# Squares of the queries as a moving operand: float32r products with a column of ones, and a transfer that turns the sums into columns

## The chip, the cores and the metric

The kernel runs on one core of a Trainium2 chip. The metric is the device time of one execution in microseconds. TensorE (PE) multiplies: it loads a stationary operand (PEld, weights of up to 128 x 128) and streams a moving operand of up to 512 columns through it into a PSUM bank. VectorE (DVE), ScalarE (ACT) and GpSimd (POOL) do the elementwise work, and SyncE (SP) issues most transfers. Each engine executes its own instructions in order and waits on semaphores for the others.

## The reference, cut to what matters

A layer of an encoder is applied to a prompt of 1024 tokens and a sample of 256 tokens. The part that the change touches is the gated delta rule: convolved and SiLU-activated queries, keys and values, four heads of 128 channels, normalised queries and keys, a recurrence in each direction, and a norm over each head's output.

```python
q = l2norm(heads(q, DN_DK))          # q * rsqrt(sum(q*q) + EPS)
...
o_f = gated_delta_chunked(q, k, v, g_f, beta_f)
o_b = flip(gated_delta_chunked(flip(q), flip(k), flip(v), flip(g_b), flip(beta_b)))
o = jnp.transpose(o_f + o_b, (0, 2, 1, 3))
o = rmsnorm(o, norm_w) * jax.nn.silu(gate.reshape(bsz, seq, DN_HEADS, DN_DV))
```

The output of the recurrence is linear in the query, and a norm follows. The kernel therefore leaves the query unscaled and carries its sum of squares, `ssq`, into the norm's epsilon: the norm needs the mean of o squared plus EPS times (128 times) the query's own sum of squares plus its epsilon. So one number per token and head is wanted: the sum over 128 channels of the query squared.

## The kernel before, in words

Activations lie with channels on the 128 partitions and tokens along the free dimension. Large projections are made in three products of split operands: `split` writes a rounded float32r copy (`hi`, ACT) and the remainder (`lo`, VectorE or GpSimd), and `mm3` multiplies hi by hi, hi by lo and lo by hi. Products of the recurrence itself are in plain f32.

The recurrence is done in five batches of 8 blocks of 128 tokens: bi = 0 to 3 are the heads of the prompt, bi = 4 the four heads of the sample. Each batch is a generator, `dn_batch`, that runs beside the main work: the projections of the convolution (`conv_tile`), of the gates (`gate_tile`, `gate_pair`) and, for the last batch, of the memory (`mem_k`, `mem_v`). A planner (`Trunk`) interleaves them in the program text. It keeps a clock that each product advances by its estimated time (`mm`: columns / 2.4 ns for float32r with at least 256 columns, four times that for f32, 2 ns for an f32 product of one column). A side generator yields a number of ns, and is continued when the clock has gone that far. TensorE executes in the order of this text (`manual_schedule`); the order of the other engines is made by the framework's scheduler from the data that each instruction needs, so an instruction on ACT or VectorE may stand earlier or later than its place in the text.

Within a batch, in order of the text:

1. decays from `grd` (L759 to L777), in the buffers `gb0` and `gb1`, which become the two directions' matrices X;
2. the blocks of 32 of the triangular inverse, by VectorE alone (L838, L841), between round trips through DRAM that rearrange them (`xsd`, `usd`, `vsd`); L844 copies the result out for the transfers L850 and L851;
3. values and keys transposed (L864, L867), and the flag "vw" that lets the main work go on;
4. the squares of the queries (L871 to L879): in each of two halves ACT squares 128 x 512 (L874), the generator yields SQ = 1800, and four f32 products take the squares as the stationary operand and the column `one` as the moving one, which gives the sums as columns, tokens on the partitions. VectorE adds the epsilon and scales (L879);
5. X[0] becomes X[0] + X[1] (L884); four buffers of the inverse are cleared (L889); SP brings back the 32 x 32 blocks (L897, L898 into `uc`, L901 and L902 into `UTm` and `Um`, L905 into `U`); after 2500 ns ACT copies `uc` into the odd blocks of `UTm` and `Um` (L911) and, after EXP / 2 = 2000 ns (in batch 0 another 5500), into `U` (L914); after another 2000 ns come the products of the inverse's two levels. The first of them takes X[0] and `UTm` (in the profile bank<-UT,gb), VectorE masks it (L924), the next takes `Um` (bank<-UT,zt), and VectorE adds it to `U` (L932). Between the levels `Mt` takes the buffer `gb1` (L943), is transposed, and fills the new `UTm` and `Um` (L950, L952);
6. the scan over the blocks, and then the norm: L1032 combines the sums of squares of the output with `ssq`, three Newton steps take the root, and the planner leaves ROOT = 2500 ns (16000 in batch 3) before the scaled output is used.

The buffers `gs` (three of 128 x 514) are shared: by the convolution's tanh (L693), its sample block (L688, L690), the evacuation of the gates (L1051, written to DRAM from there), the squares, and the final output. Weights come by SP (`load`, L135) into `raw` and are split by ACT (L125) and VectorE (L126). ACT takes the projections out of PSUM for the convolution (L723, L727, L731) and starts it (L688); VectorE continues it (L690, L695).

Of the kernel before, what the change touches and what calls it, by code (L numbers as in the profile page):

```python
# [8 lines left out]
F32 = mybir.dt.float32  # L9
F32R = mybir.dt.float32r  # L10
I32 = mybir.dt.int32
AF = mybir.ActivationFunctionType
ALU = mybir.AluOpType
# [4 lines left out]
P = 128  # L18
D = 1024
KT = D // P  # L20
NP, NS = 1024, 256
# [5 lines left out]
EPS = 1e-6  # L27
# [14 lines left out]
def f32(ap):  # L42
    return ap.bitcast(F32)


def quad(ps):
    return ps.rearrange("p (c t) -> p c t", t=P)
# [7 lines left out]
class Trunk:  # L55
# [44 lines left out]
    def mm(self, out, l, r, start=True, stop=True, more=False):  # L100
        n = 1
        for x in out.shape[1:]:
            n *= x
        if l.dtype == F32R:
            self.clock += max(n, 16) / 2.4 * (1 if n >= 256 else 4)
        else:
            self.clock += (4 * n / 2.4) if n > 1 else 2
        self.nc.tensor.matmul(out, l, r, start=start, stop=stop, skip_group_check=more)  # L108
# [10 lines left out]
    def tr(self, out, x, ident):  # L119
        self.clock += 64  # L120
        self.nc.tensor.transpose(out, x, ident)  # L121
# [42 lines left out]
def trunk_kernel(ctx: ExitStack, tc: tile.TileContext, a):  # L164
    nc = tc.nc
    V, S, G, T, SY = nc.vector, nc.scalar, nc.gpsimd, nc.tensor, nc.sync
    K = Trunk(ctx, tc, a)
    mm, mm3, tr, split = K.mm, K.mm3, K.tr, K.split

    def pool(name, bufs=1, **kw):  # L170
        if kw.get("space") != DRAM:
            kw["reuse_waits"] = "tile"
        return tc.tile_pool(name=name, bufs=bufs, **kw)
# [7 lines left out]
    dp = ctx.enter_context(pool("dram", space=DRAM))  # L181
# [5 lines left out]
    n = 0  # L187
# [29 lines left out]
    one = cst[:, C_ONE : C_ONE + 1]  # L217

    def bank(p=pq, tag="b"):
        return p.tile([P, 512], F32, tag=tag, name="bank")  # L220
# [4 lines left out]
    def rsqrt(y, x, scratch):  # L225
        V.tensor_scalar(out=y.bitcast(I32), in0=x.bitcast(I32), scalar1=-0.5, scalar2=float(0x5F3759DF), op0=ALU.mult, op1=ALU.add)
        for _ in range(3):
            V.scalar_tensor_tensor(out=scratch, in0=y, scalar=-0.5, in1=x, op0=ALU.mult, op1=ALU.mult)
            V.tensor_tensor(out=scratch, in0=scratch, in1=y, op=ALU.mult)
            V.scalar_tensor_tensor(out=y, in0=scratch, scalar=1.5, in1=y, op0=ALU.add, op1=ALU.mult)  # L230
# [167 lines left out]
    squares = hp.tile([P, 4, 1024], F32, tag="lo0", name="squares")  # L398
# [5 lines left out]
    parts = []  # L404
    for k in range(0, KT, 2):
        sq = xp.tile([P, 512], F32, tag="nacc" if k == 0 else "nsq", name="first", bufs=2 if k == 0 else 3)
# [6 lines left out]
    ms, y = pb[:, :NS], pb[:, NS : 2 * NS]  # L413
    parts = [t[:, i * NS : (i + 1) * NS] for t in parts for i in range(2)]
# [10 lines left out]
    hi, lo = x_h[2]  # L425
    rooms = [bank() for _ in range(3)]
    los = []
    for k in range(KT):
        if k in (5, 7):
            t = xp.tile([P, 512], F32, tag="nsq", name="nt", bufs=3)[:, :NS]  # L430
        else:
            at = min(k, 5)
            t = rooms[at % 3][:, at // 3 * NS : at // 3 * NS + NS]
# [3 lines left out]
        while los and (k == KT - 1 or los[0][0] < k):  # L437
            n, t = los.pop(0)
# [229 lines left out]
    qp = des.enter_context(pool("dn"))  # L668


    for i, (x, y) in enumerate(((0, 2), (1, 3), (0, 1), (2, 3))):
        V.scalar_tensor_tensor(out=mine[:, i : i + 1], in0=bdm[:, x : x + 1], scalar=-1.0, in1=bdm[:, y : y + 1], op0=ALU.mult, op1=ALU.subtract)
    def gs():
        return qp.tile([P, 514], F32, tag="gs", name="gs", bufs=3)

    def conv_tile(kind, h, out):
# [6 lines left out]
        def conv(raw, dst, n):  # L683
            for j in range(5):
                wj = sm[:, wc + j : wc + j + 1]
                src = raw[:, j : j + n]
                if j == 0:
                    S.activation(dst, src, AF.Copy, scale=wj)  # L688
                else:
                    V.scalar_tensor_tensor(out=dst, in0=src, scalar=wj, in1=dst, op0=ALU.mult, op1=ALU.add)  # L690
                yield CONV
            t = gs()[:, :n]
            S.activation(t, dst, AF.Tanh, scale=0.5)  # L693
            yield CONV
            V.scalar_tensor_tensor(out=dst, in0=t, scalar=1.0, in1=dst, op0=ALU.add, op1=ALU.mult)  # L695

        def after():
            for b, n in ((0, 510), (1, 514)):
                while len(raws) <= b:
                    yield 300  # L700
                yield from conv(raws[b], acc[:, 510 * b : 510 * b + n], n)
            out.append(quad(acc))
            while len(raws) < 3:
                yield 300
            smp = gs()[:, :NS]
            yield from conv(raws[2], smp, NS)
            SY.dma_start(sqd[kind, h], smp)
# [9 lines left out]
        for b, (t0, n) in enumerate(BLOCKS):  # L717
# [11 lines left out]
            else:  # L729
                raw = new_raw(0, 258)  # L730
                S.activation(raw[:, 2 : 2 + n], ps, AF.Copy)  # L731
                raws.append(raw)

    xsd = [dp.tile([2, 8, 4, 32, 32], F32, name=f"xsd{i}") for i in range(5)]
    usd = [dp.tile([2, 2, 8, P, 2, 16], F32, name=f"usd{i}") for i in range(5)]
    vsd = [dp.tile([2, 2, 8, 64, 2, 32], F32, name=f"vsd{i}") for i in range(5)]

    def big(tag, bufs=1):
        return qp.tile([P, 8, P], F32, tag=tag, name=tag, bufs=bufs)

    flags = set()
# [5 lines left out]
    def dn_batch(bi, qkv, chains):  # L747
# [4 lines left out]
        q2, k2 = qkv[:2]  # L752
# [29 lines left out]
        ssk, ssq, r, scr, r2, iv = (cw[:, i] for i in (0, 1, 2, 3, 6, 7))  # L782
# [4 lines left out]
        for b in range(8):  # L787
            V.scalar_tensor_tensor(
                out=junk, in0=pg[b // 4][:, (b % 4) * P : (b % 4 + 1) * P], scalar=1.0, in1=ident, op0=ALU.mult, op1=ALU.mult,
# [23 lines left out]
        X = dec  # L813
# [20 lines left out]
        for i in range(30, -1, -1):  # L834
            n, c = 32 - i, (i + 1) // 2
# [3 lines left out]
                out=t3, in0=u3[:, c:, i:],  # L839
                in1=XL[:, 32 * i + i : 32 * i + 32].unsqueeze(1).to_broadcast([P, m, n]), op=ALU.mult)  # L840
# [27 lines left out]
            yield 1000  # L868
        flags.add(("vw", bi))

        pc = bank()  # L871
        for hf in range(2):
            sq = quad(gs()[:, :512])
            S.activation(sq, q2[:, 4 * hf : 4 * hf + 4, :], AF.Square)  # L874
            yield SQ
            for c in range(4):
                n = 4 * hf + c
                mm(pc[:, n : n + 1], sq[:, c, :], one)
        V.tensor_scalar(out=ssq, in0=pc[:, :8], scalar1=4.0 * EPS, scalar2=EPS * P, op0=ALU.add, op1=ALU.mult)  # L879

        V.tensor_tensor(out=X[0], in0=X[0], in1=X[1], op=ALU.add)  # L884
        Xs = X[0]
        U = [big(f"U{d}") for d in range(2)]
        Um, UTm = big("UT1"), big("UT0")
# [11 lines left out]
        for s in (0, 2):  # L899
            c = slice(16 * s, 16 * s + 16)  # L900
            SY.dma_start(own(UTm, s), vsd[bi][1, 0][:, c].rearrange("b c h j -> (c h) b j"))  # L901
            SY.dma_start(own(Um, s), vsd[bi][0, 1][:, c].rearrange("b c h j -> (c h) b j"))  # L902
        for s in range(4):
            c = slice(16 * s, 16 * s + 16)
# [14 lines left out]
        for level, mask in enumerate((m64, m128)):  # L919
            for hf, hs in enumerate(halves):  # L920
                pz = bank()
                for c in range(4):
                    mm(pz[:, c * P : (c + 1) * P], Xs[:, hs.start + c, :], UTm[:, hs.start + c, :])
                V.tensor_tensor(out=zts[:, hf], in0=quad(pz), in1=mask.unsqueeze(1).to_broadcast([P, 4, P]), op=ALU.mult)  # L924
                yield LEV
            yield LEV
            for hf, hs in enumerate(halves):
                pu = bank()
                for c in range(4):
                    mm(pu[:, c * P : (c + 1) * P], zts[:, hf, c, :], Um[:, hs.start + c, :])  # L930
                for d in range(2):
                    V.scalar_tensor_tensor(  # L932
                        out=U[d][:, hs, :], in0=quad(pu), scalar=mine[:, 2 * level + d : 2 * level + d + 1], in1=U[d][:, hs, :],
                        op0=ALU.mult, op1=ALU.add)
                yield LEV
            if level:
                break

            Mt, Um, UTm = big("gb1"), big("UT1"), big("UT0")
            lo64, hi64 = slice(0, 64), slice(64, P)  # L940
            for hs in halves:
                for q, d in ((lo64, 0), (hi64, 1)):
                    S.activation(Mt[q, hs, :], U[d][q, hs, :], AF.Copy)  # L943
                yield LEV
            yield LEVT
            for hs in halves:
                pt = bank()
                for c in range(4):
                    tr(pt[:, c * P : (c + 1) * P], Mt[:, hs.start + c, :], ident)
                S.activation(UTm[:, hs, :], quad(pt), AF.Copy)  # L950
                for q, d in ((lo64, 1), (hi64, 0)):
                    G.tensor_copy(Um[q, hs, :], U[d][q, hs, :])  # L952
                yield LEV
            yield LEV
# [72 lines left out]
        sso, ms, t_ = cw[:, 4], cw[:, 5], cw[:, 19]  # L1027
        for b in range(8):
            junk = sq128("vt", 4)
            S.activation(junk, o[:, b, :], AF.Square, accum_out=sso[:, b : b + 1])  # L1030
            yield 250
        V.scalar_tensor_tensor(out=ms, in0=sso, scalar=1.0 / P, in1=ssq, op0=ALU.mult, op1=ALU.add)  # L1032
        rsqrt(t_, ms, sso)
        yield ROOT[bi]
        V.tensor_tensor(out=o, in0=o, in1=t_.unsqueeze(2).to_broadcast([P, 8, P]), op=ALU.mult)
# [633 lines left out]
    for h in range(HEADS):  # L1669
# [26 lines left out]
        if h == HEADS - 1:  # L1696
# [12 lines left out]
            for b in range(3):  # L1709
                hi, lo = o_h[b]  # L1710
# [5 lines left out]
    op = OutProj(o_h, h3)  # L1716
# [664 lines left out]
FILL = ((0, 0, 5), (0, 0, 4), (0, 0, 4), (0, 0, 0))  # L2381
FIRST = 12000
LANE = 1.05
SQ, EXP, LEV, LEVT, SCAN = 1800, 4000, 500, 1000, 1000
SC1, SC2, SC3 = 1200, 700, 700
TAIL, ROOT, FIRST_EXP = 3000, (2500, 2500, 2500, 16000, 2500), 5500
YA = 4500
# [88 lines left out]
```

## Time and profile before

| what | us |
|---|---|
| median of three runs | 2191.11 (2189.59 to 2192.89) |
| the profiled execution, its own time | 2190.45 |
| its span, first to last instruction | 2188.7 |
| ACT busy in the span | 879.9 |
| VectorE busy in the span | 1354.3 |

Granted TensorE clock: 0.999 of full speed over the span. The lines of the page and of the trace are shown in the prediction, each where it is used. In a group's line "x80 | 9.5, 239" means eighty instructions, 9.5 us busy in total and 239 ns the mean of one. In a timeline a line is start, length, engine, line of the kernel, operation, output and inputs, count, and in brackets how long the engine had been idle and what ended that. The names of tiles are those of the program's allocations: `gs` is also the square, `cst` the column `one`, `acc` the convolution's output, `UT` is `UTm` or `Um`, `gb` is X.

### The profile page before, as it was taken

The numbers are of one execution on the slowest core, as the hardware profiler recorded it, in microseconds if no ns is written. First come the engines' busy times: TensorE is split into PE (matmuls) and PEld (weight loads), VectorE is DVE, ScalarE is ACT, GpSimd is POOL, SyncE is SP. The second block draws the span as 40 slices with busy tenths as digits, with TensorE's granted clock in tenths as the row PEclk, the third lists the DMA queues.
The fourth block names the chain that finished last, engine by engine and source line by source line (L and its number), as shares of the span: only waits on it lengthen the run. The fifth ranks groups of instructions, "written<-read, shape, count | busy, mean of one in ns | idle before, by whom it ended". The sixth has DMA issues, their size and how long they took to land.

```text
span 2188.7 us, 32379 instructions
## 1 busy us (share of the span) xinstructions
PE 2174.0 (99%) x12436; PEld 1905.0 (87%) x12436; DVE 1354.3 (62%) x2614; ACT 879.9 (40%) x1649; POOL 569.7 (26%) x379
## 2 busy tenths in 40 slices
PE   9999999999999999999999999999999999999998
PEld 8988888898888899888988888888888888888888
DVE  7867587686874855677644556644434444378575
ACT  6533262544535553224544533332322323343454
POOL 2010010100000000142412332566666665200031
PEclk9999999999999999999999999999999999999999
DMA  5221412323234546741512521222222222493631
GB/s 194 92 93 58 119 56 91 81 66 93 75 118 126 168 139 202 243 147 39 192 67 97 171 100 63 102 84 87 82 77 78 84 97 92 143 349 120 206 111 58
DMA packets 188309, 255.13 MB, mean 117 GB/s; under 512 B 71978, under 2 KB 102266, under 8 KB 188154
## 3 DMA queue, kind: packets, MB, share of 16 engines
q1 hardware_dynamic: 170618, 228.15, 31.7%
q10 hardware_dynamic: 17536, 24.91, 3.1%
q8 instruction: 97, 1.59, 0.3%
q14 instruction: 58, 0.48, 0.1%
HBM read 179.05 MB, written 73.97 MB: 116 GB/s over the span
## 4 chain that ended last, share of the span: by engine, by line
PE 92%; DVE 5%; ACT 2%; DMA 1%; issue 1%; SPq 0%; POOL 0%; DVEq 0%; ACTq 0%
PE bank L108 91%; PE bank L121 1%; DVE acc L690 1%; DVE U L932 1%; DMA braw<-gq 1%; DMA raw<-in_w_sv 0%; DVE zt L924 0%; ACT U L914 0%; ACT UT L911 0%; DVE nt L289 0%; DVE gb L811 0%; DVE gs L690 0%; ACT junk L513 0%; ACT acc L688 0%; DVE lo L126 0%
## 5 line engine op out<-in xcount | busy, mean ns | idle before, releaser
L108 PE MATMUL bank<-hi,whi 128*128 128x512 f32 (+1 forms) x1976 | 701.2, 355 | 0.2 <-DVE vg L489 0.2
L108 PE MATMUL bank<-lo,whi 128*128 128x512 f32 (+1 forms) x1976 | 686.8, 348 | 0.0
L108 PE MATMUL bank<-hi,wlo 128*128 128x512 f32 (+1 forms) x1976 | 686.8, 348 | 0.0
L108 PEld LDWEIGHTS bank<-hi,wlo 128*128 128x128 f32 x1976 | 373.6, 189 | 48.2
L108 PEld LDWEIGHTS bank<-hi,whi 128*128 128x128 f32 x1976 | 374.4, 189 | 44.4 <-DVE vg L489 1.0
L108 PEld LDWEIGHTS bank<-lo,whi 128*128 128x128 f32 x1976 | 374.5, 190 | 42.8
L125 ACT ACTIVATE whi<-raw 128x1024 fp32r<-128x1024 f32 (+1 forms) x136 | 136.9, 1009 | 248.6 <-PE bank L108 218.9
L126 POOL TENSOR_TENSOR wlo<-raw,whi 128x1024 fp32r<-128x1024 f32 x65 | 158.4, 2439 | 295.5 <-ACT whi L125 295.5
L108 PE MATMUL bank<-bhl,whi 128*128 128x512 f32 x408 | 125.9, 390 | 0.0
L126 DVE TENSOR_TENSOR wlo<-raw,whi 128x1024 fp32r<-128x1024 f32 (+1 forms) x71 | 80.7, 1139 | 70.5 <-ACT whi L125 70.3
L126 POOL TENSOR_TENSOR wlo<-x,whi 128x1024 fp32r<-128x1024 f32 x40 | 96.5, 2412 | 47.5 <-ACT whi L125 47.5
L2107 DVE TENSOR_TENSOR x<-x,bank 128x512 f32<-128x512 f32 x21 | 14.5, 689 | 125.1 <-ACT x L1902 125.1
L690 DVE SCALAR_TENSOR_TENSOR acc<-craw,sm,acc 128x510 f32<-128x510 f32 (+1 forms) x96 | 73.8, 769 | 27.6 <-ACT acc L688 25.9
L108 PEld LDWEIGHTS bank<-bhl,whi 128*128 128x128 f32 x408 | 76.4, 188 | 16.4 <-ACT whi L125 0.4
L1915 DVE SCALAR_TENSOR_TENSOR t<-t,x 128x512 f32<-128x512 f32 x42 | 63.9, 1520 | 28.4 <-ACT t L1914 28.4
L125 ACT ACTIVATE whi<-x 128x1024 fp32r<-128x1024 f32 (+1 forms) x48 | 49.2, 1025 | 77.2 <-PE bank L108 69.3
L108 PE MATMUL bank<-bhl,wlo 128*128 128x512 f32 x204 | 79.6, 390 | 0.5 <-DVE wlo L126 0.5
L108 PE MATMUL bank<-bhl,ahl 128*128 128x512 f32 x312 | 75.0, 395 | 0.0
L1924 DVE SCALAR_TENSOR_TENSOR t<-bank,t 128x512 f32<-128x512 f32 (+1 forms) x44 | 24.5, 558 | 81.4 <-PE bank L108 81.4
L1051 ACT ACTIVATE gs<-bank 128x512 f32<-128x512 f32 (+1 forms) x60 | 31.2, 519 | 103.2 <-PE bank L108 93.8
L1902 ACT ACTIVATE x<-bank 128x512 f32<-128x512 f32 x63 | 37.7, 599 | 82.8 <-PE bank L108 80.1
L108 PEld LDWEIGHTS bank<-bhl,ahl 128*128 128x128 f32 x312 | 58.7, 188 | 13.7
(416 smaller groups left out, 4513.5 us busy)
## 6 DMA issues: line engine op xcount, KB each, us to landing
raw<-in_w_gu SPq DMA_DIRECT2D x44, 512.0 KB, 3.4
braw<-gq SPq DMA_DIRECT2D x14, 1024.0 KB, 6.4
raw<-in_w_g SPq DMA_DIRECT2D x20, 512.0 KB, 3.3
gq<-t SPq DMA_DIRECT2D x33, 256.0 KB, 2.0
gtd<-gs ACTq DMA_DIRECT2D x32, 256.0 KB, 2.4
w<-in_w_dn SPq DMA_DIRECT2D x8, 1024.0 KB, 11.0
raw<-in_w_qkv SPq DMA_DIRECT2D x12, 512.0 KB, 3.5
gq<-r SPq DMA_DIRECT2D x22, 256.0 KB, 2.0
```

Of the source, the lines that this page charges most:

```text
L108: self.nc.tensor.matmul(out, l, r, start=start, stop=stop, skip_group_check=more)
L121: self.nc.tensor.transpose(out, x, ident)
L125: self.last_hi = self.nc.scalar.activation(hi, src, AF.Copy).ins
L126: (eng or self.nc.vector).tensor_tensor(out=lo, in0=src, in1=f32(hi), op=ALU.subtract)
L690: V.scalar_tensor_tensor(out=dst, in0=src, scalar=wj, in1=dst, op0=ALU.mult, op1=ALU.add)
L932: V.scalar_tensor_tensor(out=U[d][:, hs, :], in0=quad(pu), scalar=mine[:, 2 * level + d : 2 * level + d + 1], in1=U[d][:, hs, :], op0=ALU. ...
L1051: S.activation(t, ps, AF.Tanh, scale=0.5)
L1902: S.activation(t, ps, AF.Copy)
L1915: V.scalar_tensor_tensor(out=t, in0=t, scalar=1.0, in1=src, op0=ALU.add, op1=ALU.mult)
L1924: V.scalar_tensor_tensor(out=out, in0=u, scalar=sign, in1=t, op0=ALU.mult, op1=ALU.mult)
L2107: V.tensor_tensor(out=c22, in0=c22, in1=pe, op=ALU.add)
```

## The change

The squares become a side generator of their own, `squares`, started after the sum of X. Per half ACT writes the square rounded to float32r (`hi`), GpSimd computes the square in f32 and then the remainder (`lo`), both into the buffer `gb1` that the sum of X has freed. Two float32r products take `hi` and `lo` as the moving operand, 512 columns, with a float32r column of ones as the stationary one; the sums come out as one row. ACT scales the row by EPS * 128 into a `gs` buffer, SP writes it to DRAM (`ssd`), and after the second half SP reads it back as columns into `ssq`. A flag "squares" holds the batch before `Mt` takes `gb1`. SQ becomes 3500. The constant part of the epsilon, formerly added at L879, is added behind L1032.

```diff
+    one_r = qp.tile([P, 1], F32R, name="one_r")
+    V.tensor_copy(one_r, one)
...
+    ssd = dp.tile([5, NP], F32, name="ssd")
...
-        pc = bank()
-        for hf in range(2):
-            sq = quad(gs()[:, :512])
-            S.activation(sq, q2[:, 4 * hf : 4 * hf + 4, :], AF.Square)
-            yield SQ
-            for c in range(4):
-                n = 4 * hf + c
-                mm(pc[:, n : n + 1], sq[:, c, :], one)
-        V.tensor_scalar(out=ssq, in0=pc[:, :8], scalar1=4.0 * EPS, scalar2=EPS * P, op0=ALU.add, op1=ALU.mult)
...
         V.tensor_tensor(out=X[0], in0=X[0], in1=X[1], op=ALU.add)
+        def squares():
+            parts = qp.tile([P, 1024], F32R, tag="gb1", name="q2hl")
+            hi, lo = parts[:, :512], parts[:, 512:]
+            for hf in range(2):
+                src = q2[:, 4 * hf : 4 * hf + 4, :].rearrange("p c t -> p (c t)")
+                sq = gs()[:, :512]
+                S.activation(hi, src, AF.Square)
+                G.tensor_tensor(out=sq, in0=src, in1=src, op=ALU.mult)
+                G.tensor_tensor(out=lo, in0=sq, in1=f32(hi), op=ALU.subtract)
+                yield SQ
+                pc = bank()[:1, :]
+                for t in (hi, lo):
+                    mm(pc, one_r, t, t is hi, t is lo)
+                row = gs()[:1, :512]
+                S.activation(row, pc, AF.Copy, scale=EPS * P)
+                SY.dma_start(ssd[bi, 512 * hf : 512 * hf + 512].unsqueeze(0), row)
+            SY.dma_start(ssq, ssd[bi].rearrange("(c p) -> p c", p=P))
+            flags.add(("squares", bi))
+
+        K.side(squares())
...
+            yield from wait_for("squares", bi)
             Mt, Um, UTm = big("gb1"), big("UT1"), big("UT0")
...
         V.scalar_tensor_tensor(out=ms, in0=sso, scalar=1.0 / P, in1=ssq, op0=ALU.mult, op1=ALU.add)
+        V.tensor_scalar(out=ms, in0=ms, scalar1=4.0 * EPS * EPS * P, scalar2=None, op0=ALU.add)
...
-SQ, EXP, LEV, LEVT, SCAN = 1800, 4000, 500, 1000, 1000
+SQ, EXP, LEV, LEVT, SCAN = 3500, 4000, 500, 1000, 1000
```

## The prediction

> **What bounds the kernel now.** I read the page first: busy times, then the chain that ended last.
>
> ```profile
> span 2188.7 us, 32379 instructions
> ...
> PE 2174.0 (99%) x12436; PEld 1905.0 (87%) x12436; DVE 1354.3 (62%) x2614; ACT 879.9 (40%) x1649; POOL 569.7 (26%) x379
> ...
> PE 92%; DVE 5%; ACT 2%; DMA 1%; issue 1%; SPq 0%; POOL 0%; DVEq 0%; ACTq 0%
> ```
>
> TensorE is busy for 99% of the span and carries 92% of the chain. A change is therefore worth the TensorE time that it removes, less the TensorE waits that it makes. The five batches of the recurrence lie between 260 and 850 us, and the table of windows shows no room there either:
>
> ```profile
> 260.00:850.00 590.00, 588.30 (x3741) 528.60 (x3740) 409.82 (x1043) 279.63 (x686) 34.24 (x78) 1.00 0.35 102
> ```
>
> Columns: window, length, then busy time of PE, PEld, DVE, ACT and POOL, granted clock, DMA share, GB/s. TensorE lacks 1.7 us of 590 at full clock; POOL has 34 us of work. Next, TensorE's timeline in the third batch (bi = 2), around the products that change:
>
> ```profile
> 532.36 0.40 PE L108 MATMUL bank<-hi,wlo 128*128 128x512 f32 x1
> 532.59 0.95 PE L108 MATMUL bank<-cst,gs 128*128 128x1 f32 x8
> 533.41 0.47 PE L108 MATMUL bank<-hi,whi 128*128 128x512 f32 x1
> 533.72 0.39 PE L108 MATMUL bank<-lo,whi 128*128 128x512 f32 x1
> 533.95 0.40 PE L108 MATMUL bank<-hi,wlo 128*128 128x512 f32 x1
> ...
> 535.57 0.95 PE L108 MATMUL bank<-cst,gs 128*128 128x1 f32 x8
> ...
> 544.17 1.05 PE L108 MATMUL bank<-UT,gb 128*128 128x128 f32 x8
> ```
>
> Read starts, not durations, since products overlap. Two 512-column products follow each other at 533.95 - 533.72 = 0.23 us. The eight records of a half's four f32 products (two records each) begin at 532.59, and the second product behind them at 533.72: 1.13 us, of which one ordinary step is 0.23, so a half costs 0.90 us. A line of the groups by form confirms the count, 80 records = 5 batches x 2 halves x 8:
>
> ```profile
> L108 PE MATMUL bank<-cst,gs 128*128 128x1 f32 x80 | 9.5, 239 | 0.0
> ```
>
> **The change, part by part.** *Products.* Removed: 10 halves x 0.90 = 9.0 us. Added: per half two float32r products with 512 moving columns and one stationary column. No row has one stationary column; the nearest one is the 512-column step above, 0.23 us. Bounds: 0.23 (pipelined, one column loaded no slower than 128) and 0.40, the whole record, if they do not overlap. I take 0.23, since such steps hold through the whole timeline. Added 10 x 0.455 = 4.55 us; net -4.45 us, at worst 9.0 - 8.0 = -1.0.
>
> *Side work.* Each half's f32 square on ACT becomes a float32r square of the same size and a copy of one row of 512:
>
> ```profile
> L874 ACT ACTIVATE gs<-acc x10: 615/622/632, 263.8 to 778.8; 128x512 f32<-128x512 f32 x10
> L879 DVE TENSOR_SCALAR cw<-bank x5: 166/167/167, 269.5 to 787.4; 128x8 f32<-128x8 f32 x5
> L884 DVE TENSOR_TENSOR gb<-gb,gb x5: 1217/1220/1228, 216.4 to 729.2; 128x1024 f32<-128x1024 f32 x5
> ```
>
> Triples are min/median/max ns. The row copy is bounded by 0.62 us; ten are 6 us of ACT beside a 590 us stretch with 280 busy, so I count nothing for their sum. VectorE's small operation moves from L879 to behind L1032: 0.17 us before and after, hidden behind the 2.5 us planned before its result is used; `one_r` is smaller still. Moving the sum of X ahead of the squares costs nothing: its first run is at 216.4 us, 47 us ahead of the first square at 263.8. POOL gets two operations of 128x512 per half, nearest rows:
>
> ```profile
> L126 POOL TENSOR_TENSOR lo<-nt,hi 128x512 fp32r<-128x512 f32 x11 | 15.1, 1379 | 58.3 <-ACT hi L125 58.2
> ...
> L1784 POOL TENSOR_TENSOR x<-raw 128x512 f32<-128x512 f32 x20 | 26.1, 1308 | 7.0 <-DVE x L1875 5.5
> ```
>
> A pair is 1.31 + 1.38 = 2.7 us. The planner leaves 3500 ns; it counts 213 ns where the chip takes 0.23, so this is about 3.7 us. The pair is just hidden; without that cover each microsecond of lateness is one of TensorE.
>
> *Transfers.* SP issues three more per batch: two rows of 2 KB, and a read back of 1024 runs of 4 bytes that waits for both. Behind them on SP stand weight loads:
>
> ```profile
> q1 hardware_dynamic: 170618, 228.15, 31.7%
> 547.50 0.35 SPq L135 DMA_DIRECT2D raw<-in_w_g  x1
> DMA to landing us min/median/max: 1.7/3.5/4.2
> ```
>
> (The last line is of the tile `uc`.) From the first: 31.7% of 16 engines x 2188.7 us over 170618 packets is 65 ns per packet, so 1024 take about 4.2 us over 16 engines, an estimate. Bounds of the cost to TensorE: nothing, or a load 4 us late per batch. I take nothing: `ssq` is read only behind the scan, and the next load is issued at 547.5, after the inverse's first products.
>
> *The moved part.* Before, two yields of 1800 stood in the batch's own path; now squares are a side of their own. The first product of the inverse (bank<-UT,gb) comes sooner in TensorE's fixed order by the time from one yield before the first block to the end of the second: 2 x (535.57 - 532.59) = 6.0 us. What feeds it doesn't come sooner by that. These ACT lines stand ahead of it in batch 2:
>
> ```profile
> 539.43 0.60 ACT L727 ACTIVATE craw<-bank 128x512 f32<-128x512 f32 x1 [1.38 <-PE bank L108]
> 540.05 0.48 ACT L911 ACTIVATE UT<-uc 32x256 f32<-32x256 f32 x1
> 540.56 0.72 ACT L688 ACTIVATE acc<-craw,sm 128x514 f32<-128x514 f32 x1
> 541.31 1.45 ACT L911 ACTIVATE UT<-uc 32x256 f32<-32x256 f32 x3
> ```
>
> The product needs the first two L911, done at 541.31 + 0.48 = 541.79; before, at 544.17, 2.4 us were in hand. ACT is in order and L727 waits for TensorE's convolution block. That comes earlier by the two removed blocks less one new pair, 1.80 - 0.455 = 1.35 us. The product thus gains 6.0 - 1.35 = 4.6 us on its inputs, has 2.4 in hand, and TensorE waits 2.2 us. The other batches:
>
> ```profile
> 281.69 1.46 ACT L911 ACTIVATE UT<-uc 32x256 f32<-32x256 f32 x3
> 283.27 1.05 PE L108 MATMUL bank<-UT,gb 128*128 128x128 f32 x8
> ...
> 410.45 1.45 ACT L911 ACTIVATE UT<-uc 32x256 f32<-32x256 f32 x3
> 414.67 1.05 PE L108 MATMUL bank<-UT,gb 128*128 128x128 f32 x8
> ...
> 671.42 1.47 ACT L911 ACTIVATE UT<-uc 32x256 f32<-32x256 f32 x3
> 675.03 1.05 PE L108 MATMUL bank<-UT,gb 128*128 128x128 f32 x8
> ...
> 790.88 1.97 ACT L911 ACTIVATE UT<-uc 32x256 f32<-32x256 f32 x4
> 795.24 1.05 PE L108 MATMUL bank<-UT,gb 128*128 128x128 f32 x8
> ```
>
> In hand are 1.1, 3.7, 3.1 and 3.4 us for batches 0, 1, 3 and 4, so waits of 3.5, 0.9 and 1.5 in the first three. In batch 4 the transfers come last:
>
> ```profile
> 787.81 0.82 SPq L897 DMA_DIRECT2D uc<-usd  x2
> ...
> 789.80 0.44 SPq L901 DMA_DIRECT2D UT<-vsd  x1
> ```
>
> They don't move with TensorE at all, so the wait is 6.0 - 3.4 = 2.6 us. All five: 3.5 + 0.9 + 2.2 + 1.5 + 2.6 = 10.7 us. The low end: ACT may be given L911 ahead of L727. In batch 2 the last `uc` transfer was issued at
>
> ```profile
> 533.12 0.45 SPq L898 DMA_DIRECT2D uc<-usd  x1
> ```
>
> and with the median landing of 3.5 us is there near 537, while the product would come at 538.2. Then batches 1 to 3 wait for nothing, batch 0 about 0.6 and batch 4 still 2.6: 3.2 us. Batch 0's 3.5 is the softest term, because a weight split between its L911s can't stay there once the product is early. I take 6 us, near the middle, and keep 3.2 and 10.7.
>
> The new wait for "squares" stands behind the inverse's first level. By the plan the squares end at about 2 x 3.5 = 7 us, and the batch is there after 2.5 + 2 + 2 + 2.5 = 9 us, so it costs nothing; behind it would be ACT's write of `Mt` into the same buffer, then the transposes.
>
> **Sum**, against the profiled execution's own 2190.45 us (span 2188.7 and 1.75 around it): 2190.45 - 4.45 + 6 = **2192.0 us**. That execution is 0.66 us below the median of 2191.11, too little to correct for.
>
> **Rivals.** *No new wait* (24%): ACT and SP are reordered so that the inputs follow the product; 2190.45 - 4.45 = 2186.0, or 2189 with only batch 4's wait. For it: the sum of X ran far ahead of its place in the text, so the order isn't that of the text. Against it: in batch 2 ACT held L911 behind L727 until 540.05 although `uc` was there near 537.
>
> *POOL comes late* (16%): the products wait for `lo`. The mechanism is POOL against VectorE:
>
> ```profile
> L1915 DVE SCALAR_TENSOR_TENSOR t<-t,x x42: 679/694/2483, 1389.2 to 1901.2; 128x512 f32<-128x512 f32 x42
> ```
>
> This two-input operation takes 694 ns at the median and 2483 at most, beside POOL work of the same stage. If each operation of a pair stands behind one such VectorE operation, the pair takes 2.7 + 2 x 0.7 = 4.1 us against 3.7, and a queued POOL operation of another kind adds about as much again. At 1 us late, the first half's lateness takes the place of the wait at the inverse, the second half's is new: 5 x 1 = 5 us, 2197. It decides when a pair ends more than 3.7 us after its squares are asked for. The Trainium skill, SBUF — State Buffer, section "SBUF: two separate sides", says that VectorE with two SBUF inputs and a reading GpSimd operation take a shared port in turns, for whole instructions. The row's spread agrees; by that rule taken at its full price the sum would be near this rival's, by the median row near mine.
>
> *The saving isn't there* (10%): one-column products don't overlap, -1.0 instead of -4.45: 2195.5. For it, only that no such product is in the trace.
>
> **How the numbers follow.** My forecast, new waits of 3.2 to 10.7 us that eat the saving, has 50% and spans 2189 to 2196. About 0.2% (4.4 us) is what a measurement can tell from no change, so faster means below 2186.7 and slower above 2195.5. Faster: most of the first rival, 18%. Slower: nearly all of the second, half of the third, the forecast's end, 23%. The same: 59%. The range is 2185 to 2199.5, from the first rival to beyond the second.
>
> **What would show it.** Right: records of 128x512 with a one-column weight at steps of 0.23 us, twenty of them; before bank<-UT,gb in each batch a gap on TensorE whose releaser is ACT L911 or a transfer, longest in batches 0 and 4. Wrong: those gaps are missing (first rival), gaps stand before the new products with POOL as releaser (second), or the new steps are 0.4 us (third). A late weight split behind the read back would show transfers that I counted at nothing.

## The result, and the profile after

| | median, us | lowest to highest | runs |
|---|---|---|---|
| before | 2191.86 | 2189.59 to 2192.89 | 6 |
| after | 2204.27 | 2201.19 to 2204.59 | 6 |

The ratio is 1.0059, with a 95% interval of 1.0048 to 1.0069: the changed kernel is 12.4 us slower. The time forecast was 2192.0 us and the range ended at 2199.5, so it holds neither the median nor any single run. The profiled execution after took 2203.6 us, 13.15 more than the one before.

The page of after, the lines that answer to those of before:

```profile
span 2201.8 us, 32361 instructions
...
PE 2175.8 (99%) x12376; PEld 1902.7 (86%) x12376; DVE 1359.7 (62%) x2615; ACT 886.0 (40%) x1659; POOL 595.4 (27%) x399
```

TensorE has 60 records fewer: 80 of the old products went and 20 of the new came. Yet it is busy for 1.8 us more, a first sign that it ran slowly somewhere. The table of windows, same columns as in the prediction, for the five batches:

```profile
260.00:850.00 590.00, 576.60 (x3597) 514.17 (x3596) 410.48 (x1033) 282.02 (x689) 58.79 (x96) 0.99 0.35 97
```

Before, TensorE lacked 1.7 us of these 590; now it lacks 13.4. The view of waits (total us, times, longest), for TensorE in the same stretch, first after:

```profile
PE bank L108 <- ACT UT L922: 11.2, 5, 5.6
PE bank L108 <- ACT stage L1166: 1.1, 1, 1.1
```

and before:

```profile
PE bank L108 <- DVE U L932: 1.0, 1, 1.0
```

L922 is the old L911, the copy of `uc` into the inverse's operand. Three more waits after, all under 0.5 us, sum to 0.9. TensorE's timeline after, the inverse's first product in batches 0 to 4, with the idle time in brackets:

```profile
279.29 1.51 PE L108 MATMUL bank<-UT,gb 128*128 128x128 f32 x8 [2.08 <-ACT UT L922]
...
415.50 1.16 PE L108 MATMUL bank<-UT,gb 128*128 128x128 f32 x8 [1.73 <-ACT UT L922]
...
546.21 1.16 PE L108 MATMUL bank<-UT,gb 128*128 128x128 f32 x8 [1.53 <-ACT UT L922]
...
674.35 1.16 PE L108 MATMUL bank<-UT,gb 128*128 128x128 f32 x8 [0.30 <-ACT UT L922]
...
795.99 2.08 PE L108 MATMUL bank<-UT,gb 128*128 128x128 f32 x8 [5.58 <-ACT UT L922]
```

These are the gaps that the prediction's last paragraph asked for, with the releaser that it named. Eight such products take 1.05 us before and 2.08 us in batch 4 after. The windows around them say why; the number after the five busy times is the granted clock:

```profile
279.00:282.00 3.00, 2.71 (x15) 2.71 (x16) 2.79 (x4) 2.89 (x7) 0.00 (x0) 0.66 0.53 126
282.00:285.00 3.00, 3.00 (x22) 3.00 (x21) 1.98 (x3) 0.81 (x2) 0.10 (x1) 0.77 0.00 0
...
796.00:799.00 3.00, 3.00 (x13) 2.60 (x14) 0.00 (x0) 2.00 (x5) 0.00 (x0) 0.50 0.53 86
799.00:802.00 3.00, 3.00 (x15) 2.90 (x14) 0.75 (x2) 1.67 (x4) 0.00 (x0) 0.50 0.53 195
```

TensorE is busy through them, at 0.50 to 0.77 of full speed. Time lost is length times what lacks to 1: 3 x 0.34 + 3 x 0.23 = 1.7 us in batch 0, 6 x 0.50 = 3.0 us in batch 4, together 4.7 us. No such window is in this stretch of the trace of before.

An account of the profiled executions: waits 11.2 + 1.1 + 0.9 - 1.0 = 12.2, low clock 4.7, products about -4.3 (experiment 3 below): 12.6 us, where 13.15 were measured.

### The profile page after: what moved, and what is told of

Its sections match the earlier page's. It is cut to its first block, busy times and chain, and to the rows that moved or that the text cites. A ratio compares the mean times of both kernels' runs of the same rounds, so it can differ in the third digit from the quotient of the medians.

```text
span 2201.8 us, 32361 instructions
## 1 busy us (share of the span) xinstructions
PE 2175.8 (99%) x12376; PEld 1902.7 (86%) x12376; DVE 1359.7 (62%) x2615; ACT 886.0 (40%) x1659; POOL 595.4 (27%) x399
## 4 chain that ended last, share of the span: by engine, by line
PE 62%; DMA 1%; DVE 1%; ACT 0%; SPq 0%; issue 0%; DVEq 0%; ACTq 0%
PE bank L108 61%; DMA braw<-gq 1%; PE bank L121 0%; DVE lo L126 0%; DMA vsd<-W 0%; SPq L855 0%; SPq L854 0%; DVE bhl L126 0%; DMA uc<-usd 0%; ACT hi L125 0%; DVE nacc L254 0%; DVE xs L2305 0%; DVE wlo L126 0%; ACT bhl L125 0%; ACT whi L125 0%
## 5 line engine op out<-in xcount | busy, mean ns | idle before, releaser
L883 POOL TENSOR_TENSOR gs<-acc 128x512 f32<-128x512 f32 x10 | 13.0, 1303 | 216.2 <-DVE W L845 78.6
```

The lines of the kernel that those rows point to most:

```text
L883: G.tensor_tensor(out=sq, in0=src, in1=src, op=ALU.mult)
```

## The experiments

Two theories stood against each other. **A**: the loss comes from the batch's own path, which became two yields shorter, so that the inverse's first product is due before its inputs. **B**: it comes from what was added: GpSimd's pair, the transfers, the one-column products.

**1. The path gets its length back.** All of the change stays; only the batch waits 2 x 1800 ns again.

```diff
         K.side(squares())
+        yield 3600
```

> The changed kernel with the 3600 ns put back into the batch's own path behind the start of the squares; nothing else differs. Theory A (the loss is TensorE waiting for the inverse's inputs, because its first product moved up 6 us): the waits ahead of bank<-UT,gb shrink from 2.3, 1.9, 1.7, 0.5 and 5.8 us to under 1 us each, the clock stays at full speed, and the saving of the products is left: 2191.9 - 4.45 = about 2187 us, at most 2190. Theory B (the loss comes from the added work: two GpSimd operations per half, the row copies on ScalarE, three transfers on SP): it stays at 2200 to 2204 us.

Measured: 2187.76 us (2186.85 to 2189.26), the kernel before beside it 2191.05, ratio 0.9985 (0.9976 to 0.9994). TensorE's waits and the inverse in batch 4:

```profile
PE bank L108 <- DVE U L944: 0.4, 2, 0.2
```

```profile
791.04 1.07 PE L108 MATMUL bank<-UT,gb 128*128 128x128 f32 x8
```

The waits for ACT are gone, and one line turns the loss into a gain of 3.3 us. So the new form of the squares is itself worth 3.3 us (1.3 to 5.3 by the interval), and A holds. This version is faster than both kernels.

**2. The shorter path alone.** The squares of before, f32 on ACT and four f32 products, are made a side like in the change; no float32r, no GpSimd, no row, no transfer.

```diff
+        def squares():
+            for hf in range(2):
+                sq = quad(gs()[:, :512])
+                S.activation(sq, q2[:, 4 * hf : 4 * hf + 4, :], AF.Square)
+                yield SQ
+                pc = bank()
+                for c in range(4):
+                    mm(pc[:, c : c + 1], sq[:, c, :], one)
...
+            flags.add(("squares", bi))
+        K.side(squares())
```

> The kernel before with its own f32 products of one moving column, but run as a side beside the inverse with SQ = 3500, the sum of X ahead of them; no float32r squares, no GpSimd work, no row, no transfer. Theory A: the waits ahead of the inverse are there as in the changed kernel, and the products cost 4.45 us more than its: 2204 + 4 = about 2205 to 2209 us. Theory B: without the added work the time is that of before, 2190 to 2194 us.

Measured: 2209.72 us (2208.31 to 2210.8), ratio 1.0084 (1.0071 to 1.0098): slower than before by 18.7 us with none of the added parts. TensorE's waits:

```profile
PE bank L108 <- ACT UT L911: 6.0, 1, 6.0
PE bank L108 <- issue: 5.5, 4, 1.5
```

The four of "issue" stand at the same product in the other batches; their releaser isn't shown. The time is 0.7 us above the upper end that A gave and far from B's 2190 to 2194, so B falls as the cause of the loss. The clock falls here too, in batches 2, 3 and 4. Waits of 12.1 us (with one of 0.6 more) against 1.0 before, and a half clock over 3.4, 3.4 and 6.9 us of TensorE's work, make 18.0 of the 18.7 us. As an example batch 3, whose product starts at 676.55 after a gap of 1.0 us:

```profile
676.00:679.00 3.00, 2.45 (x21) 2.48 (x22) 0.16 (x1) 2.92 (x7) 0.00 (x0) 0.98 0.37 111
679.00:682.00 3.00, 3.00 (x16) 3.00 (x16) 1.38 (x2) 0.36 (x1) 0.00 (x0) 0.50 0.51 175
```

**3. What the old squares cost.** Before, with the squares and their products left out: a constant stands in `ssq`, and the 3600 ns stay.

```diff
-        pc = bank()
...
+        V.memset(ssq, 128.0 * EPS)
+        yield 3600
```

> The kernel before without the queries' squares: the products, their ACT squares and the sum are left out, a constant stands in for the sum, and the 3600 ns stay in the path. It prices the first term of the sum, ten blocks of 0.90 us: 2191.2 - 9.0 = 2182.2 us, from 2180.5 to 2184, with nothing else moved. If a block costs only its 0.2 us of columns beyond what neighbours hide, the time stays above 2187. The run with the path put back (2187.8) then leaves 5.6 us for the ten new pairs, against 4.6 in the sum.

Measured: 2182.56 us, ratio 0.9964 (0.9951 to 0.9978) to 2190.26. By the medians ten blocks cost 7.7 us, by the interval 4.8 to 10.7, so the 9.0 of the prediction is not contradicted. The trace is sharper. A product of the main work that stands behind eight of the ten blocks, at 771.60 us before, stands here at

```profile
763.93 0.48 PE L108 MATMUL bank<-mhi,whi 128*128 128x512 f32 x1
```

That is 7.67 us sooner, of which 0.11 us were there ahead of the batches: 0.94 us a block, near the 0.90 read from the starts. The new ones are read from the trace of after, a pair and the next product of the main work:

```profile
786.91 0.63 PE L108 MATMUL bank<-q2hl,one_r 128*1 128x512 f32 x2
787.38 0.28 PE L108 MATMUL bank<-whi,mhi 128*128 128x256 f32 x1
```

A pair takes 0.47 us. The saving is 9.0 - 4.7 = 4.3 us with blocks of 0.90, 4.7 us with 0.94; both lie inside the interval of experiment 1.

**4. GpSimd's pair.** Experiment 1 without the pair, the remainder and its product: the remainder of the squares' rounding is left out of the sum.

```diff
-                G.tensor_tensor(out=sq, in0=src, in1=src, op=ALU.mult)
-                G.tensor_tensor(out=lo, in0=sq, in1=f32(hi), op=ALU.subtract)
...
-                for t in (hi, lo):
-                    mm(pc, one_r, t, t is hi, t is lo)
+                mm(pc, one_r, hi)
```

> The run with the path put back in all batches, and of the squares only the rounded part: the two GpSimd operations, the remainder and the second product of each half are left out. If the GpSimd pair is hidden, as the sum has it, only ten products of 0.23 us go: 2187.8 - 2.3 = 2185.5 us, from 2184 to 2187. If the pair still costs TensorE waits or VectorE its port, more goes, down to 2182.6, the time without any squares.

Measured: 2186.74 us, ratio 0.998 (0.9971 to 0.9989), 1.0 us below experiment 1, while ten products fewer at 0.23 us are worth 2.3; the two intervals overlap, so the difference is not resolved. It shows nothing that the pair costs.

**5. Only batch 4 gets its length back**, since it has half of the waiting.

```diff
         K.side(squares())
+        if bi == 4:
+            yield 3600
```

> The changed kernel with the 3600 ns put back in the last batch alone (bi = 4). Theory A, with most of the loss in batch 4 (TensorE's offset against before grows by about 9 us there and by 4 in the four others together): 2204.3 - 9 - 1 = about 2194 us, from 2193 to 2197, and the waits of batches 0 to 2 stay near 2 us each. Theory B: no change, 2203 to 2205.

Measured: 2197.83 us (2195.71 to 2199.44), ratio 1.003 (1.0019 to 1.004), 0.8 us above the upper end expected. The waits (L924 is L922, moved by the added lines):

```profile
PE bank L108 <- ACT UT L924: 7.4, 5, 2.1
PE bank L108 <- ACT stage L1168: 1.6, 1, 1.6
```

Batch 4 still waits, 1.7 us. It begins as soon as batch 3 is done, and with batches 0 to 3 shortened it begins sooner in the plan: its first transposes stand behind 2781 products of the main work after, behind 2808 before.

**6. Which of the two makes batch 4 late.** A1: its own path. A2: its early start. In the first kernel only batch 3 gets its length back, in the second all but batch 4.

```diff
+        if bi == 3:      # first kernel
+        if bi < 4:       # second kernel
+            yield 3600
```

> The changed kernel with the 3600 ns put back in batch 3 alone. Theory A2 (batch 4 loses twice: by its own 3600 ns, and because batch 3, done sooner in the plan, lets batch 4 begin 27 products of 256 columns sooner, while VectorE's chain of the 32 x 32 blocks comes no sooner): the transposes of batch 4 stand again where they stood before (main product 2808, not 2781), the wait ahead of its bank<-UT,gb falls from 5.8 to about 2.6 us, the clock stays up there, and the time falls by 6 to 8 us to 2196 to 2198. Theory A1 (batch 4's wait is its own 3600 ns alone): its wait stays between 5 and 6 us and the time falls by the 0.5 us of batch 3's wait, to 2203 or 2204.

> The changed kernel with the 3600 ns put back in batches 0 to 3, not in batch 4. A2: only the predicted wait of batch 4 is left, 6.0 us moved less 3.4 in hand = 2.6 us: 2187.8 + 2.6 = 2190.4, from 2189 to 2192. A1: batch 4 loses as in the changed kernel, 5.8 us of waiting and the low clock behind it: 2195 to 2197.

Measured: the first 2200.28 us (2198.96 to 2203.89), ratio 1.0043; the second 2195.13 us (2194.0 to 2196.94), ratio 1.0017 (1.0008 to 1.0025). In the first, batch 4 begins behind 2808 products again, and its wait falls from 5.6 to 4.7 us only; its time lies between the two forecasts, since batch 3's own wait of 0.3 us and 2.0 us of smaller waits go as well. In the second all waits for the copies are gone but this (three other waits are of 0.4 to 0.5 us):

```profile
PE bank L108 <- ACT UT L924: 4.7, 1, 4.7
```

So the early start accounts for about 1 us of the wait, the own path for the rest: A1. Beside experiment 1, batch 4's path alone costs 2195.13 - 2187.76 = 7.4 us, of which 4.7 is the wait. The rest is the clock:

```profile
790.60:796.80 6.20, 6.20 (x27) 5.71 (x28) 1.15 (x3) 3.37 (x7) 0.00 (x0) 0.50 0.43 127
```

6.2 us at half speed lose 3.1 us. Together that is 7.8 us, where 7.4 were measured.

**7. Half of the length in every batch**, to see if the loss is in proportion.

```diff
         K.side(squares())
+        yield 1800
```

> The changed kernel with 1800 ns, half of what was taken out, put back in all batches. If the waits follow the path's length, they are those of the sum with 3.9 us moved in place of 6.0: batch 0 about 1.4, batches 1 to 3 nearly none, batch 4 between 0.5 and 2.5 by how much sooner it begins: 2187.8 + 2 to 4 = 2190 to 2192. If the loss comes from anything that doesn't scale with the path: near 2204 or near 2188.

Measured: 2197.5 us (2195.21 to 2198.42), ratio 1.0026 (1.0016 to 1.0036); 2190 to 2192 had been expected. The main waits:

```profile
PE bank L108 <- DMA U<-vsd: 5.1, 1, 5.1
PE bank L108 <- DVE zt L936: 1.2, 2, 0.8
```

Batches 0 to 3 no longer wait for ACT's copies, batch 4 waits nearly as long as with nothing given back, here for a transfer. That is no measure of proportion, because the product did not move half way. In TensorE's order it stands behind 2889 products of the main work; before it was 2934, in experiment 1 2925, after 2862, and 2892 with nothing given back in batch 4 alone (second kernel of experiment 6). The earlier start of the batch, behind 2790 products instead of 2808, took what the 1800 ns gave.

**8. The gap filled.** If the low clock comes from the gap, products of zeros in it should keep it up. `hold(n, room)` issues n f32 products of 512 columns that nobody reads. One kernel is the changed one with six of them, the other the second kernel of experiment 6 with five, both in batch 4 ahead of the inverse's first product.

```diff
             for hf, hs in enumerate(halves):
+                if bi == 4 and level == 0 and hf == 0:
+                    hold(6, bank())
                 pz = bank()
```

> The changed kernel with six f32 products of zeros by zeros, 512 columns, ahead of the first product of the inverse in batch 4; they compute nothing that is used and take about 0.84 us each, 5.0 us. If the low granted clock (0.50 for 6 us behind the wait of 5.6 us) is itself a part of the loss: the wait is filled, the clock stays near 1.00 and the time falls by about 3 us to 2201. If the clock row is only a sign of the wait and costs nothing: 2204 or, with dummy work not hidden in the wait, up to 2209.

> The run with the path put back in batches 0 to 3 (2195.1 us, one wait of 4.9 us in batch 4, granted clock 0.66 and 0.77 in the two stretches of 6 us behind it), and in that wait five f32 products of zeros by zeros, 4.2 us, whose result nothing reads. If the low clock is a part of the price of the wait, 6 x 0.34 + 6 x 0.23 = 3.4 us: it stays at 1.00 and the time falls to about 2192. If only the wait counts: 2195 to 2196.

Measured: 2202.42 us (2201.52 to 2202.8), ratio 1.0051 (1.0038 to 1.0065), and 2193.29 us (2192.65 to 2197.49), ratio 1.0014 (1.0005 to 1.0023) to 2190.26. The clock does stay up. The window behind the gap in the first kernel:

```profile
794.00:797.00 3.00, 3.00 (x22) 2.44 (x21) 0.00 (x0) 2.46 (x6) 0.00 (x0) 1.00 0.51 99
```

In time the gain is too small to tell: 1.0059 and 1.0051, 1.0017 and 1.0014 have overlapping intervals, and both times lie between their two forecasts. (The 3.4 us in the second expectation are 3.1, since its first stretch holds 2.6 us of the gap itself.) In the traces the main product that stood at 791.15 us before comes 4.4 and 2.2 us sooner than in the unfilled kernels; 1.5 of the 4.4 is that the inverse's product itself starts sooner, at 794.52 instead of 795.99. Later waits differ (a `wlo` of VectorE near 1400 us costs 1.2 us in both filled kernels and nothing in the unfilled), so part of it is lost again. That the gap pulls the clock down is shown; what those microseconds are worth at the end stays open.

## Why the prediction was wrong

**The products**, -4.45 us: direction right, and the traces bear the size out. The new pair was put at 0.455 us and measured 0.47. The old block, read as 0.90 us from its starts, was worth 0.94 in the trace where it is taken out. The net is -4.3 to -4.7 us in the traces; in time experiment 1 has -3.3 (-1.3 to -5.3), too wide to tell it from -4.45.

**Side work, GpSimd's pair, transfers**, at nothing: right as far as the runs reach. No TensorE wait in the five batches names POOL or `ssd` (one of 0.9 us for POOL, at L389, is in both traces), and experiments 1 and 4 show no cost of the pair. The read back landed 4.7 us after its issue where 4.2 were estimated.

**The moved part**: the mechanism was right, and the step that failed is "I take 6 us, near the middle". The prediction's terms added up to 10.7, and L922 cost 11.2. That these two lie so close is luck, as the terms by batch below show. The low end rested on "ACT may be given L911 ahead of L727". That did not happen. ACT's timeline after, batch 2:

```profile
541.39 0.60 ACT L730 ACTIVATE craw<-bank 128x512 f32<-128x512 f32 x1
541.89 0.57 ACT L890 ACTIVATE gs<-bank 1x512 f32<-1x512 f32 x1
542.36 0.61 ACT L882 ACTIVATE q2hl<-acc 128x512 fp32r<-128x512 f32 x1
...
543.61 0.48 ACT L922 ACTIVATE UT<-uc 32x256 f32<-32x256 f32 x1
544.60 1.06 ACT L125 ACTIVATE whi<-raw 128x1024 fp32r<-128x1024 f32 x1 [0.51 <-PE bank L108]
545.68 1.45 ACT L922 ACTIVATE UT<-uc 32x256 f32<-32x256 f32 x3
```

L730, the old L727, is still ahead of the copies. Between the two that the product needs there is now also a weight split that itself waits for TensorE. The second copy ends at 545.68 + 0.48 = 546.16, the product starts at 546.21. The prediction held that in batch 0 a weight split between the copies can't stay there once the product is early. In batch 0 it did go, and the wait was 2.1 us instead of 3.5; here one has come in. The new row copy and the second square (L890, L882) stand ahead of the copies too, but ACT then waits 0.51 us for TensorE before the split, so they don't set the time here.

**The terms by batch.** Foreseen 3.5, 0.9, 2.2, 1.5 and 2.6; measured 2.1, 1.7, 1.5, 0.3 and 5.6. Batches 0 to 3 are below their sum (5.6 of 8.1), batch 4 is at twice its term. Its step was "They don't move with TensorE at all, so the wait is 6.0 - 3.4 = 2.6 us". In the second kernel of experiment 6, where nothing else has gone wrong yet, that says where it fails:

```profile
789.57 1.94 ACT L924 ACTIVATE UT<-uc 32x256 f32<-32x256 f32 x4
...
790.59 1.65 PE L108 MATMUL bank<-UT,gb 128*128 128x128 f32 x6 [4.69 <-ACT UT L924]
```

The product was due at about 790.59 - 4.69 = 785.9, not 6.0 but 9.3 us ahead of the 795.24 of before; its inputs came only 790.88 - 789.57 = 1.3 us sooner: 9.3 - 1.3 - 3.4 = 4.6, the wait. The 3.3 us beyond 6.0 are the gain itself: the main work ahead of this place is 3.1 us sooner in this kernel (the product that stood at 771.60 us before), and the inputs are not. Of these 3.1 us 0.5 were there already at 200 us, ahead of all batches; the rest is TensorE time that the squares of the earlier batches saved. In experiment 1 the saving, and a place in TensorE's order nine products of the main work sooner (2925 instead of 2934, an estimated 9 x 0.12 = 1.1 us), used up what was in hand:

```profile
789.92 1.96 ACT L923 ACTIVATE UT<-uc 32x256 f32<-32x256 f32 x4
```

Two copies are done at 789.92 + 0.98 = 790.90 and the product starts at 791.04, with 0.1 us left of 3.4.

In after it is the other way round. The product was due at 795.99 - 5.58 = 790.41, 4.8 us sooner than before, and the inputs came later. In TensorE's order it stands 72 products of the main work sooner. The shorter path makes 42 of them (second kernel of experiment 6), which take 5.9 us before, as the prediction's 6.0 has it; the other 30 go with the batch's earlier start, which the prediction didn't have. The inputs:

```profile
793.13 0.80 SPq L908 DMA_DIRECT2D uc<-usd  x2
```

```profile
794.91 1.03 ACT L922 ACTIVATE UT<-uc 32x256 f32<-32x256 f32 x2 [4.79 <-DMA uc<-usd]
```

794.91 against 790.88 is 4.0 us, and 4.8 + 4.0 - 3.4 = 5.4. The transfers wait for VectorE's blocks of the inverse, and their copy out by ACT is 5.8 us later, the main work at that place only 3.7. Rows of before (a product of the main work, and L844), then of after (the same product, and L848):

```profile
771.60 0.48 PE L108 MATMUL bank<-mhi,whi 128*128 128x512 f32 x1
...
777.18 1.18 ACT L844 ACTIVATE UT<-W 128x512 f32<-128x512 f32 x1 [1.69 <-DVE W L841]
```

```profile
775.26 0.39 PE L108 MATMUL bank<-mhi,whi 128*128 128x512 f32 x1
...
782.99 1.13 ACT L848 ACTIVATE UT<-W 128x512 f32<-128x512 f32 x1 [3.75 <-DVE W L845]
```

The copy fell behind the main work by 2 us, though batch 4 had been begun sooner in the plan: the plan moves TensorE's instructions, and the chain on VectorE didn't follow. VectorE has hardly an idle moment there; after, for one, this weight split stands inside the chain:

```profile
774.65 0.56 DVE L845 TENSOR_REDUCE W<-W 128x14 f32<-128x392 f32 x1
775.13 1.22 DVE L126 TENSOR_TENSOR wlo<-raw,whi 128x1024 fp32r<-128x1024 f32 x1
776.26 1.43 DVE L842 TENSOR_TENSOR W<-W,UT 128x406 f32<-128x406 f32 x1
```

Which of VectorE's other work made it late has not been tested.

**The clock** was not in the sum. A wait was priced at its own length, and the half speed behind it added 4.7 us to 11.2. This is the second step that failed: with 10.7 in place of 6 the sum gives only 2196.7 us, and without the 4.7 the profiled execution would by this account have taken about 2198.9, inside the range.

**The rivals.** "No new wait" is out for the change as made. Experiment 1 shows that price, 2186.0 forecast and 2187.76 measured, for a path of the old length. "POOL comes late" did not occur: GpSimd's pair took 1.16 + 1.56 = 2.7 us at the medians, as foreseen. "The saving isn't there" did not occur either.

The miss is 13.15 - 1.55 = 11.6 us on the profiled execution: 5.2 of L922 (11.2 instead of 6), 4.7 of the clock, 1.0 of other waits (1.1 + 0.9 - 1.0), 0.1 of the products (4.3 instead of 4.45) make 11.0; 0.6 us stay open.

## What to carry to other kernels

When work leaves a path whose length was also a delay, the delay goes with it: count what was in hand at the next join, subtract the move and also every microsecond that the change saves ahead of it, and put the delay back if the result is negative. If your own sum of terms says 10.7, a smaller value needs a row that shows the relief, not only the possibility of it. On a saturated TensorE a wait can cost more than its length: here 1.7 us of half clock followed a gap of 2.1 us, though not in every kernel, and about 3 us gaps of 4.7 to 5.6 us.

## What the runs showed of the hardware that was not expected

The granted clock falls behind gaps shorter than expected, and not every time. Behind the unfilled gaps of 4.7 to 6.0 us in batch 4 it fell in all five kernels that have one. After 2.08 us in batch 0 it fell to 0.66 over the window shown above; in the kernel of experiment 5 the same gap, 2.08 us, left it untouched:

```profile
279.00:282.00 3.00, 2.85 (x25) 2.85 (x26) 2.65 (x4) 2.89 (x7) 0.10 (x1) 1.00 0.55 138
```

In experiment 2 the gaps of batches 0 to 3 are 1.47, 1.48, 1.48 and 1.04 us; the clock stayed full behind the first two and fell behind the other two, to 0.50 for the last. In the profiled execution of experiment 1 it fell at 28.5 us behind a gap of 0.20 us that the kernel before has as well, with the clock left full. How long the half clock lasts can be read at its edges, here in batch 0 after:

```profile
279.50:280.00 0.50, 0.50 (x6) 0.50 (x6) 0.46 (x2) 0.49 (x2) 0.00 (x0) 0.94 0.85 344
283.00:283.50 0.50, 0.50 (x5) 0.50 (x5) 0.00 (x0) 0.00 (x0) 0.00 (x0) 0.64 0.00 0
```

With 0.50 in all windows between, it begins at 279.94 and ends at 283.36: 3.4 us. In batch 4 it lasts 6.8 us in the same way (795.4 to 802.2), and in experiment 2 10.2 us, so one, two and three times the same length. The Trainium skill, TensorE: Matmul & The Clock Gate, section "What's actually happening", describes a half clock that is decided over a free-running window of about 3.4 us; its "Why this matters for your kernels" asks for no idle gaps above some 3 us. The half clock agrees with the 0.50 and the window with the 3.4 us, and a window that runs freely would fit that equal gaps end differently. The limit of 3 us was no protection here: gaps from 1.0 us on were followed by it. What decides whether a short gap is followed by it, no run here shows.
